# Gates in one go, 112 candidate sums, 896 dense columns: one change to the expert stage of a two-block transformer kernel

## The chip, the cores and the metric

The kernel runs on one core of a Trainium2 chip. A time is the device time of one execution in microseconds; a comparison uses the median of several executions on the same chip. The time before is 2967.11 us (median of 3 runs, 2965.75 to 2971.43). The profile comes from one more execution, of 2963.08 us, whose span from the first to the last instruction is 2961.3 us.

## The reference, cut to what matters

One sequence of 256 tokens, 2048 channels, goes through a mixer block, a gated feed-forward block, a second mixer, and then the part that is changed: a layer of 16384 experts, of which every token uses 8 heads x 16. Each expert is a row of `expert_u` and a row of `expert_v`.

```
s1, s2 = scores of 128 half keys each, per token and head
v1, i1 = top_k(s1, 16);  v2, i2 = top_k(s2, 16)
cand = v1[:, None] + v2[None, :]            # 256 sums
vs, ci = top_k(cand, 16)
eidx = i1[ci // 16] * 128 + i2[ci % 16];  gates = softmax(vs)
act  = gelu(expert_u[eidx] . x)             # 128 experts a token
h    = h + sum_k (act * gates)[k] * expert_v[eidx[k]]
h    = h + sigmoid(rms_norm(h) @ w_ple_gate) * (p @ w_ple_proj)
```

Both lists `v1` and `v2` are sorted, so a sum at place (i, j) has (i + 1)(j + 1) - 1 sums ahead of it that are no smaller, and only places with (i + 1)(j + 1) <= 16 can be among the 16 largest.

## The kernel before, in words

Everything is one program, written as generators ("lanes") that are stepped by the loops that issue the main products. The order in which a step issues its instructions is fixed when the program is built, and each engine runs its own instructions in that order. `lanes.step()` steps all five lanes; it is called once for each weight chunk (`next_chunk`) and in the waiting loops (`until`). `beside()` steps lanes 2 to 4 in the product that makes the queries. Weights come in chunks of 128 x 1024 through SP's queue into four buffers (`raw`); a chunk of the early and last products is split into a high and a low part by ACT (L349) and DVE (L350), a chunk marked `whole` is not.

The expert stage has four parts.

*Selection.* `topk` (L1586) runs twice, on lanes 2 and 3, one for the even and one for the odd heads. For a head, DVE finds the 16 best half keys of both kinds for both halves of the tokens (`top16`, L1569, on 128 scores), POOL forms the 16 x 16 sums of each token half (L1601), DVE finds the 16 best of 256 (`top16` again), POOL works out the two places from the index (L1606 to L1611), DVE compares them with a counting row (L1616), POOL multiplies by the indices (L1618), DVE sums (L1624), and POOL makes the row index (L1626 to L1628). ACT makes the exponentials of the gates of that head (L1620) and POOL scales them (L1633). `slots_` (L1636) copies the gates when all heads are done.

*The u rows.* `u_rows` (L1675) has POOL issue indirect loads (`gather`, L1661, issued at L1663) of 128 rows of `expert_u`, one row of 8 KB for each of 128 tokens, into 10 seats (4 in the second half of the tokens). DVE multiplies each with the normed token and sums (L1703). The first of these sums is issued when four heads are selected. There are 256 such loads.

*The spread of the weights.* `spots` (L1716) turns the 128 weights of a token and their indices into a dense 128 x 128 map with matmuls (L1762, L1794) and puts it into G (`put`, L1742, copies by ACT). For the second half of the tokens this is done in two halves of the map, 16 groups of 8 tokens each: the first before the dense product, the second beside it, with an accumulator pair shared by two groups.

*The v rows.* The columns of `expert_v` are cut in two. The first 1024 (`w_vd`) are done densely: 128 chunks of 128 rows, each with 8 matmuls against G (L1900). The other 1024 (`w_vs`) are gathered, 256 loads of 128 rows of 4 KB into 8 seats, and DVE adds each one, times its weight, to an accumulator `sacc` (L1840). `v_rows` (L1820) is on lane 4; in the dense loop it gets two steps a chunk, and a step issues up to two loads and one sum. Ahead of one of the steps POOL copies a column of the newest chunk (L1897), so POOL's loads wait there until that chunk has landed; a chunk's buffer is free only after this copy. At the end of each token half `turned` (L1809) transposes the sum (L1815) and DVE adds it to x (L1817): for the first half 8 steps later on lane 0, for the second half at once, within the step.

*The end.* After the dense loop DVE adds the dense sums to x (L1904); `x_block` (calling `part` and `x_square`) makes the high and low parts of the 8 dense column blocks (ACT L545, DVE L546, the squares ACT L563 and POOL L564); the product of `p` and `w_ple_proj` follows (`pp_done`, L1911); then the 8 gathered blocks are treated alike; then the last gate's product runs over the blocks 0 to 15 in that order, three matmuls for each block and output, and `g_done` (L1928) finishes and stores.

Of the kernel before, what the change touches and what calls it, by code (L numbers as in the profile page):

```python
# [6 lines left out]
F32 = mybir.dt.float32  # L7
# [5 lines left out]
OP = mybir.AluOpType  # L13
# [6 lines left out]
CH = 1024  # L20
GORD = [3, 2, 1, 0]
# [42 lines left out]
def layout(i):  # L64
# [161 lines left out]
def program(tc, A, out, stage=99, dbg=None):  # L226
# [90 lines left out]
    if stage > 3:  # L317
        add("w_pq", split=False)
        whole.update(range(len(order), len(order) + 128))
        add_kout("w_vd", 128, 0)  # L320
# [1210 lines left out]
    subk, qring, eg, ek, kk = cK(8, 2, 128), cK(4, T), cK(2, 128), cK(8, 2, 2, 16), cK(2, 128)  # L1531
    G.dma_start(subk.rearrange("p h s n -> p (h s n)"), A["subk"])
    sc = slab("sc").rearrange("p (t h s n) -> p t h s n", t=2, h=8, s=2)
    cT = Carve("cT")
    e1T, e2T, wT = sq[:, 0], sq[:, 1], acc_sq
# [50 lines left out]
    def topk(first):  # L1586

        cand, oh = cT(2, 16, 16), cT(2, 2, 16, 16)
        vv, ii, iif = cT(2, 2, 16), cT(2, 2, 16).bitcast(U32), cT(2, 2, 16)
        vs, ci, cf, c1, gs = cT(2, 16), cT(2, 16).bitcast(U32), cT(2, 16), cT(2, 2, 16), cT(2, 4)  # L1590
        xf = cT(2, 16)
        flat = lambda v: v.rearrange("p t s n -> p (t s n)")
        for h in range(first, 8, 2):
# [17 lines left out]
            G.tensor_add(c1[:, :, 1], c1[:, :, 1], cf)  # L1611
            G.tensor_scalar(gs[:, :, 0], vs[:, :, 0], -1.0, None, op0=OP.mult)
# [6 lines left out]
            for tt in range(2):  # L1619
                S.activation(eg[:, tt, hs], vs[:, tt], AF.Exp, bias=gs[:, tt, 0:1], accum_out=gs[:, tt, 1:2])  # L1620
# [4 lines left out]
            V.reciprocal(gs[:, :, 2], gs[:, :, 1])  # L1625
# [5 lines left out]
            for tt in range(2):  # L1631
                g = eg[:, tt, hs]
                G.tensor_scalar(g, g, gs[:, tt, 2:3], None, op0=OP.mult)  # L1633
            flags["heads"] = flags.get("heads", 0) + 1

    def slots_():  # L1636
# [3 lines left out]
        G.tensor_copy(gate_, eg)  # L1640
# [75 lines left out]
    def spots(tt):  # L1716
# [50 lines left out]
        else:  # L1767

            for half in range(2):
                lo, p = half * 64, None  # L1770
                for n in range(16):
# [18 lines left out]
                    if half == 0 or n % 2 == 0:  # L1790
                        p = pair("tok" if half else "sp")
                    at = 0 if half == 0 else n % 2 * 512
                    for k in range(8):
                        PE.matmul(p[:, at + k * 64:at + k * 64 + 64], Q[:, k], P[:, k, 0:64], start=True, stop=True)  # L1794
# [11 lines left out]
    vrow = [t.rearrange("p n d -> p (n d)").rearrange("p (n d) -> p n d", n=4)[:, j] for t in rows_[:2] for j in range(4)]  # L1806
    xb = {}

    def turned(t, tt, delay):  # L1809
# [3 lines left out]
        p = pair("tok")  # L1813
        for j in range(8):
            PE.transpose(p[:, j * 128:j * 128 + 128], t[:, j * 128:j * 128 + 128], ident)  # L1815
# [4 lines left out]
    def v_rows():  # L1820
# [4 lines left out]
        for n in range(256):  # L1825
# [16 lines left out]
            if s == 127:  # L1842
# [5 lines left out]
                if tt:  # L1848
                    for _ in turned(t, 1, 0):
                        pass  # L1850
# [104 lines left out]
```

## Time and profile before

| what | value |
|---|---|
| median of 3 runs | 2967.11 us |
| profiled execution, its span | 2963.08 us, 2961.3 us |
| PE busy | 2311.8 us, 78% |
| DVE busy | 1999.7 us, 68% |
| ACT busy | 1191.2 us, 40% |
| POOL busy | 900.9 us, 30% |
| moved from HBM | 757.77 MB |
| queue of SP's loads, of POOL's loads | 353.83 MB, 408.75 MB |

The expert stage takes the second half of the span, from about 1490 us on. Times in the rows are us from the span's start. A share of busy time is an average over stages with different limits; what bounds a stage is read from the windows of that stage (busy time of each engine, the granted TensorE clock, the DMA engines' share and rate) and from what ended the idle time before an instruction, which stands in brackets behind it. DMA share is the mean busy share of the 16 DMA engines. A fp32 matmul of 256 columns is recorded as two instructions.

### The profile page before, as it was taken

The page shows a single profiled execution, that of the slowest core. Times are in us where ns is not written, and L with a number is a line of the kernel's source. Part 1 is how long each engine was busy: PE and PEld are TensorE (multiplying, and loading weights), DVE is VectorE, ACT ScalarE, POOL GpSimd, SP SyncE. Part 2 cuts the span into 40 slices and gives each one's busy share as a digit, 9 for nine tenths or more (in the row PEclk, how much of TensorE's full clock was granted, in tenths as well). Part 3 has the DMA queues.
Part 4 walks back from the last instruction along what each step waited for, and adds up shares of the span by engine and source line. Part 5 has one row for each costly group of instructions (what it writes and reads, how often), then busy time and mean ns, then how long its engine had stood idle before and what let it go on. Part 6 is the DMA issues. An engine that isn't in the chain of part 4 may idle for free.

```text
span 2961.3 us, 39499 instructions
## 1 busy us (share of the span) xinstructions
PE 2311.8 (78%) x14635; PEld 2106.1 (71%) x14635; DVE 1999.7 (68%) x2615; ACT 1191.2 (40%) x2560; POOL 900.9 (30%) x1262
## 2 busy tenths in 40 slices
PE   8999999999999999999997200022222999999799
PEld 8887898888889999998986200011122988888689
DVE  5455666555556565656537999988998866666655
ACT  4355555444444454445411000058880444400043
POOL 3202215111111000331135543333334555555420
PEclk9999999999999999999998655555555799999999
DMA  6444455655655555543557799999997799999945
GB/s 221 153 128 122 134 158 180 196 188 187 197 187 190 185 180 184 172 151 109 182 201 279 291 407 422 422 397 408 415 415 317 265 403 404 395 401 409 366 148 166
DMA packets 174675, 765.11 MB, mean 258 GB/s; under 512 B 19585, under 2 KB 22049, under 8 KB 141201
## 3 DMA queue, kind: packets, MB, share of 16 engines
q1 hardware_dynamic: 99216, 353.83, 36.0%
q0 software_dynamic: 75264, 408.75, 34.5%
q8 instruction: 115, 1.88, 0.3%
q14 instruction: 80, 0.65, 0.1%
HBM read 757.77 MB, written 4.21 MB: 257 GB/s over the span
## 4 chain that ended last, share of the span: by engine, by line
PE 59%; DMA 12%; DVE 10%; issue 9%; POOL 8%; ACT 1%; another core or an unknown queue 0%; SPq 0%; POOLq 0%; DVEq 0%; ACTq 0%
PE acc L411 11%; PE acc L1900 7%; PE acc L386 6%; PE acc L388 6%; PE acc L387 6%; DMA rows<-w_vs,idx 6%; PE acc L412 6%; POOL rows L1663 5%; DMA rows<-w_u,idx 5%; DVE rows L1703 5%; PE acc L485 3%; PE acc L483 3%; PE acc L484 3%; PE sp L1794 1%; DMA raw<-w_vd 1%
## 5 line engine op out<-in xcount | busy, mean ns | idle before, releaser
L350 DVE TENSOR_TENSOR wlo<-raw,whi 128x1024 fp32r<-128x1024 f32 (+1 forms) x501 | 613.5, 1233 | 415.1 <-ACT whi L349 408.3
L349 ACT CAST whi<-raw 128x1024 fp32r<-128x1024 f32 (+1 forms) x501 | 519.7, 1042 | 380.2 <-PE acc L387 130.9
L1703 DVE SCALAR_TENSOR_TENSOR rows<-rows,yt 128x2048 f32<-128x2048 f32 x256 | 580.3, 2285 | 42.9 <-DMA rows<-w_u,idx 38.6
L1900 PE MATMUL acc<-G,raw 128*128 128x256 f32 x2048 | 457.3, 385 | 12.4 <-DMA raw<-w_vd 11.1
L1900 PEld LDWEIGHTS acc<-G,raw 128*128 128x128 f32 x2048 | 391.8, 193 | 71.7 <-DMA raw<-w_vd 17.0
L1840 DVE SCALAR_TENSOR_TENSOR sacc<-rows,sm,sacc 128x1024 f32<-128x1024 f32 x254 | 327.3, 1289 | 143.8 <-DMA rows<-w_vs,idx 127.4
L1663 POOL DMA_INDIRECT rows<-w_u,idx x256 | 244.2, 954 | 380.0 <-DVE rows L1703 274.8
L1663 POOL DMA_INDIRECT rows<-w_vs,idx x256 | 248.8, 972 | 149.6 <-DVE sacc L1840 81.7
L411 PE MATMUL acc<-xl,whi 128*128 128x512 f32 x704 | 248.2, 391 | 0.0
L411 PE MATMUL acc<-xh,whi 128*128 128x512 f32 x704 | 248.1, 391 | 0.0
L1762 PE MATMUL sp<-P,Q 128*128 128x128 f32 x256 | 60.2, 430 | 213.9 <-ACT P L1758 213.9
L1762 PEld LDWEIGHTS sp<-P,Q 128*128 128x128 f32 x256 | 55.8, 330 | 218.6 <-ACT P L1758 218.6
L564 POOL TENSOR_TENSOR acc_sq<-acc_sq,sq 128x256 f32<-128x256 f32 x63 | 57.0, 904 | 504.6 <-ACT sq L563 502.7
L485 PE MATMUL acc<-ring,wlo 128*128 128x256 f32 x704 | 199.3, 283 | 0.1
L483 PE MATMUL acc<-ring,whi 128*128 128x256 f32 x704 | 199.3, 283 | 0.1
L484 PE MATMUL acc<-ring,whi 128*128 128x256 f32 x704 | 199.2, 283 | 0.0
L412 PE MATMUL acc<-xh,wlo 128*128 128x256 f32 x704 | 197.2, 280 | 0.0
L412 PE MATMUL acc<-xl,wlo 128*128 128x256 f32 x704 | 197.1, 280 | 0.0
L1659 PE MATMUL yt<-keep,xg 128*128 128x128 f32 x32 | 5.6, 350 | 237.6 <-DVE rows L1703 237.1
L1191 POOL TENSOR_TENSOR hT<-cF 128x256 f32<-128x256 f32 x44 | 70.8, 1609 | 372.7 <-ACT whi L349 342.8
L1659 PEld LDWEIGHTS yt<-keep,xg 128*128 128x128 f32 x32 | 5.0, 184 | 238.1 <-DVE rows L1703 237.3
L386 PE MATMUL acc<-xh,whi 128*128 128x256 f32 x520 | 150.6, 290 | 3.2 <-ACT whi L349 1.8
(486 smaller groups left out, 5692.7 us busy)
## 6 DMA issues: line engine op xcount, KB each, us to landing
raw<-w_gu SPq DMA_DIRECT2D x176, 512.0 KB
raw<-w_vd SPq DMA_DIRECT2D x128, 512.0 KB
raw<-w_down SPq DMA_DIRECT2D x88, 512.0 KB
raw<-w_out SPq DMA_DIRECT2D x32, 512.0 KB
raw<-w_pq SPq DMA_DIRECT2D x32, 512.0 KB
raw<-w_pg SPq DMA_DIRECT2D x32, 512.0 KB
raw<-w_b SPq DMA_DIRECT2D x24, 512.0 KB
raw<-w_lat SPq DMA_DIRECT2D x18, 512.0 KB
```

The lines of the kernel that those rows point to most:

```text
L349: S.copy(hi[j][:, a:b], raw[j][:, a:b])
L350: V.tensor_sub(lo[j][:, a:b], raw[j][:, a:b], hi[j][:, a:b].bitcast(F32))
L386: PE.matmul(ps, wh, xh, start=start, stop=False, **k)
L411: PE.matmul(ps, wh, xh.both(k), start=k == 0, stop=False, skip_group_check=True)
L412: PE.matmul(ps[:, :T], wl, xh[:, k], start=False, stop=k == kb - 1, skip_group_check=True)
L483: PE.matmul(o, wh, ah, start=(k == 0 and j % 2 == 0), stop=False, skip_group_check=True)
L484: PE.matmul(o, wh, al, start=False, stop=False, skip_group_check=True)
L485: PE.matmul(o, wl, ah, start=False, stop=(k == nk - 1), skip_group_check=True)
L1663: G.indirect_dma_start(dst, None, src, bass.IndirectOffsetOnAxis(ap=idx[:, tt, s:s + 1], axis=0))
L1703: V.scalar_tensor_tensor(r, r, 1.0, accT, op0=OP.mult, op1=OP.mult, accum_out=wv[:, tt, s:s + 1])
L1840: V.scalar_tensor_tensor(sacc, r, w, sacc, op0=OP.mult, op1=OP.add)
L1900: PE.matmul(o, w, gs_[k // 16][:, k % 16], start=(k == 0 and j % 2 == 0), stop=k == 127, skip_group_check=True)
```

## The change

Three edits, with what they need around them.

- In `topk` the candidates are 112 sums instead of 256: the first 4 places of list 1 with all 16 of list 2, and places 4 to 15 of list 1 with the first 4 of list 2. They lie one behind the other, so POOL works out the two places from the index with more instructions. The exponentials leave `topk`: each head's 16 best sums stay in `vsa`, and `slots_` makes all gates at once.
- The dense part of `expert_v` has 896 columns (7 matmuls a chunk, chunks of 128 x 896), the gathered part 1152 (rows of 4608 bytes, 6 seats, an accumulator of three banks). The accumulator takes a bank from the pair that `spots` used in its second half, so there each group of 8 tokens has a bank and a `put` of its own.
- At the end of the second token half `turned` goes to lane 0 with a delay of 5 steps and then makes the parts of the gathered blocks (`finished`). After the dense loop, lanes 4 and 0 are finished first; the parts of the 7 dense blocks are made between the outputs of the `p` product; and the last gate's product runs over the blocks from 7 to 15 and then 0 to 6 (`Rolled`, with the rows of `w_ple_gate` rolled alike).

```diff
+KV = 7
+DV = KV * 128
+SV = 2048 - DV
-    a["w_vd"] = np.ascontiguousarray(i["expert_v_2"][0][:, :CH])
-    a["w_vs"] = np.ascontiguousarray(i["expert_v_2"][0][:, CH:])
-    a["w_pg"] = blocks(i["w_ple_gate_2"][0])
+    a["w_vd"] = np.ascontiguousarray(i["expert_v_2"][0][:, :DV])
+    a["w_vs"] = np.ascontiguousarray(i["expert_v_2"][0][:, DV:])
+    a["w_pg"] = blocks(np.roll(i["w_ple_gate_2"][0], -DV, axis=0))
...
             G.tensor_copy(iif, ii)
             for tt in range(2):
-                G.tensor_add(cand[:, tt], vv[:, tt, 0][:, :, None].to_broadcast([128, 16, 16]),
-                             vv[:, tt, 1][:, None, :].to_broadcast([128, 16, 16]))
+                for a, na, nb, at in ((0, 4, 16, 0), (4, 12, 4, 64)):
+                    G.tensor_add(cand[:, tt, at:at + na * nb].rearrange("p (a b) -> p a b", a=na), ...)
             yield
-            yield from top16([(cand[:, tt].rearrange("p a b -> p (a b)"), vs[:, tt], ci[:, tt]) for tt in range(2)])
+            vs = vsa[:, h]
+            yield from top16([(cand[:, tt], vs[:, tt], ci[:, tt]) for tt in range(2)])
             G.tensor_copy(cf, ci)
-            G.tensor_scalar(c1[:, :, 0], cf, 1.0 / 16, -7.5 / 16, op0=OP.mult, op1=OP.add)
-            G.tensor_scalar(c1[:, :, 0], c1[:, :, 0], 1.5 * 2.0 ** 23, None, op0=OP.add)
-            G.tensor_scalar(c1[:, :, 0], c1[:, :, 0], 1.5 * 2.0 ** 23, None, op0=OP.subtract)
-            G.tensor_scalar(c1[:, :, 1], c1[:, :, 0], -16.0, None, op0=OP.mult)
-            G.tensor_add(c1[:, :, 1], c1[:, :, 1], cf)
-            G.tensor_scalar(gs[:, :, 0], vs[:, :, 0], -1.0, None, op0=OP.mult)
+            i_, j_, r_ = c1[:, :, 0], c1[:, :, 1], 1.5 * 2.0 ** 23
+            G.tensor_scalar(i_, cf, 1.0 / 16, -7.5 / 16, op0=OP.mult, op1=OP.add)
+            G.tensor_scalar(i_, i_, r_, None, op0=OP.add)
+            G.tensor_scalar(i_, i_, r_, None, op0=OP.subtract)
+            G.tensor_scalar(j_, cf, 0.25, -12.375, op0=OP.mult, op1=OP.add)
+            G.tensor_scalar(j_, j_, r_, None, op0=OP.add)
+            G.tensor_scalar(j_, j_, r_, None, op0=OP.subtract)
+            G.tensor_scalar(far, cf, 1.0 / 112, -7.5 / 112, op0=OP.mult, op1=OP.add)
+            G.tensor_scalar(far, far, r_, None, op0=OP.add)
+            G.tensor_scalar(far, far, r_, None, op0=OP.subtract)
+            G.tensor_sub(j_, j_, i_)
+            G.tensor_mul(j_, j_, far)
+            G.tensor_add(i_, i_, j_)
+            G.tensor_scalar(xf, i_, 12.0, -48.0, op0=OP.mult, op1=OP.add)
+            G.tensor_mul(xf, xf, far)
+            G.tensor_scalar(j_, i_, -16.0, None, op0=OP.mult)
+            G.tensor_add(j_, j_, cf)
+            G.tensor_add(j_, j_, xf)
...
-            for tt in range(2):
-                S.activation(eg[:, tt, hs], vs[:, tt], AF.Exp, bias=gs[:, tt, 0:1], accum_out=gs[:, tt, 1:2])
...
-            V.reciprocal(gs[:, :, 2], gs[:, :, 1])
...
-            for tt in range(2):
-                g = eg[:, tt, hs]
-                G.tensor_scalar(g, g, gs[:, tt, 2:3], None, op0=OP.mult)
...
-        G.tensor_copy(gate_, eg)
+        G.tensor_copy(gs, ga[:, :, 0])
+        G.tensor_tensor(ga, ga, gs[:, :, None].to_broadcast(wide), op=OP.subtract)
+        yield
+        S.activation(ga, ga, AF.Exp)
+        for _ in range(2):
+            yield
+        V.tensor_reduce(gs, ga, axis=AX.X, op=OP.add)
+        V.reciprocal(gs, gs)
+        G.tensor_mul(gate_..., vsa, gs...)
...
-                    if half == 0 or n % 2 == 0:
-                        p = pair("tok" if half else "sp")
+                    p = bank(pairs_["tok"], "tok") if half else pair("sp")
...
-                    if half and n % 2:
-                        put(range(4, 8), t0 - 8, p, 16)
-                    elif not half:
-                        put(range(4), t0, p[:, 0:512], 8)
+                    put(range(4 * half, 4 * half + 4), t0, p[:, 0:512], 8)
...
+    def finished(which):
+        for j in which:
+            part(xb["h"][:, j], xb["l"][:, j], xb["x"][:, j], C("ple", j))
+            x_square(0 if j == KV else 1 + j % 2, xb["x"][:, j])
     def turned(t, tt, delay):
         for _ in range(delay):
             yield
-        p = pair("tok")
-        for j in range(8):
-            PE.transpose(...)
-        V.tensor_add(o, o, p.rearrange("p (k t) -> p k t", k=8))
+        for j0 in range(0, 16 - KV, 4):        # 4, 4 and 1 blocks, one bank
+            p = bank(pairs_["tok"], "tok")
+            for j in range(n):
+                PE.transpose(...)
+            V.tensor_add(o, o, p[:, :n * 128].rearrange("p (k t) -> p k t", k=n))
         yield
+        if tt:
+            finished(range(KV, 16))
...
-                    if m < 256 and m % 8 not in busy:
+                    if m < 256 and m % 6 not in busy:
...
-                if tt:
-                    for _ in turned(t, 1, 0):
-                        pass
-                else:
-                    lanes.add(0, turned(t, 0, 8))
+                lanes.add(0, turned(t, tt, 5 if tt else 8))
...
+    lanes.finish([4, 0])
...
+        if j % 2 and j // 2 < KV:              # in pp_done
+            finished([j // 2])
...
-    until("v")
-    for j in range(8, 16):
-        x_block(j, x, C("ple"), xh, xl)
...
-    project(16, 16, (xh, xl), g_done, ready=lambda: flags.get("n5"))
+    project(16, 16, (Rolled(xh), Rolled(xl)), g_done, ready=lambda: flags.get("n5"))
```

## Rows read from the trace of the kernel before

**Rows 1.** Windows: us, busy of PE, PEld, DVE, ACT, POOL, clock, DMA, GB/s

```profile
1594.00:1707.00 113.00, 44.90 (x189) 37.58 (x187) 103.76 (x261) 8.95 (x37) 59.18 (x113) 0.69 0.77 285
1707.00:2270.00 563.00, 64.11 (x273) 59.26 (x273) 520.05 (x457) 240.42 (x773) 208.61 (x223) 0.53 1.00 412
2270.00:2333.00 63.00, 56.41 (x257) 55.17 (x257) 50.03 (x50) 13.04 (x67) 42.38 (x40) 0.50 0.51 162
2333.00:2570.00 237.00, 233.77 (x1177) 207.62 (x1178) 163.40 (x136) 128.68 (x413) 126.19 (x179) 0.98 1.01 396
2570.00:2809.00 239.00, 220.09 (x1009) 189.28 (x1007) 157.75 (x124) 2.13 (x7) 123.03 (x180) 0.98 1.01 401
2841.00:2864.00 23.00, 18.67 (x136) 18.02 (x134) 20.06 (x30) 17.25 (x40) 9.09 (x12) 0.85 0.45 147
2864.00:2961.30 97.30, 90.08 (x737) 88.67 (x737) 59.37 (x82) 39.68 (x53) 7.54 (x19) 0.99 0.53 163
```

**Rows 2.** Costliest groups of the page: busy, mean ns | idle before, releaser

```profile
L1703 DVE SCALAR_TENSOR_TENSOR rows<-rows,yt 128x2048 f32<-128x2048 f32 x256 | 580.3, 2285 | 42.9 <-DMA rows<-w_u,idx 38.6
...
L1840 DVE SCALAR_TENSOR_TENSOR sacc<-rows,sm,sacc 128x1024 f32<-128x1024 f32 x254 | 327.3, 1289 | 143.8 <-DMA rows<-w_vs,idx 127.4
```

**Rows 3.** Chain of waits, four pieces: start, us, what

```profile
1702.11 88.33 DVE rows L1703 x80
...
1809.57 19.12 DMA rows<-w_u,idx
...
2341.21 13.87 PE acc L1900 x64
...
2678.57 13.68 DMA rows<-w_vs,idx
```

**Rows 4.** DVE in order of time, one head and the first row's sum

```profile
1559.83 0.85 DVE L1572 MAX8 cT<-sc 128x8 f32<-128x128 f32 x4
...
1567.99 0.74 DVE L1580 MAX8 cT<-cT 128x8 f32<-128x256 f32 x2
...
1571.62 1.22 DVE L1616 TENSOR_TENSOR cT<-cT,keep 128x1024 f32<-128x1024 f32 x1 [2.10 <-POOL cT L1611]
...
1594.08 2.27 DVE L1703 SCALAR_TENSOR_TENSOR rows<-rows,yt 128x2048 f32<-128x2048 f32 x1
```

**Rows 5.** POOL in order of time, the places of the same head

```profile
1569.59 0.21 POOL L1606 CAST cT<-cT 128x32 f32<-128x32 uint32 x1 [3.54 <-DVE cT L1583]
1569.89 0.22 POOL L1607 TENSOR_SCALAR cT<-cT 128x32 f32<-128x32 f32 x1
1570.20 0.30 POOL L1608 TENSOR_SCALAR cT<-cT 128x32 f32<-128x32 f32 x1
1570.59 0.29 POOL L1609 TENSOR_SCALAR cT<-cT 128x32 f32<-128x32 f32 x1
...
1571.34 0.25 POOL L1611 TENSOR_TENSOR cT<-cT 128x32 f32<-128x32 f32 x1
```

**Rows 6.** DVE in order of time, a later head, between two rows' sums

```profile
1642.08 2.27 DVE L1703 SCALAR_TENSOR_TENSOR rows<-rows,yt 128x2048 f32<-128x2048 f32 x1
...
1644.27 1.22 DVE L1616 TENSOR_TENSOR cT<-cT,keep 128x1024 f32<-128x1024 f32 x1
```

**Rows 7.** DVE and PE in order of time, from the last v row on

```profile
2806.12 2.62 DVE L1840 SCALAR_TENSOR_TENSOR sacc<-rows,sm,sacc 128x1024 f32<-128x1024 f32 x2 [1.10 <-DMA rows<-w_vs,idx]
...
2809.84 1.97 PE L1815 MATMUL tok<-keep,rows 128*128 128x128 f32 x8 [11.38 <-ACT rows L1847]
...
2811.60 29.77 PE L1900 MATMUL acc<-G,raw 128*128 128x256 f32 x128
...
2840.45 2.47 DVE L1904 TENSOR_TENSOR x<-x,acc 128x512 f32<-128x512 f32 x4
...
2842.84 6.56 DVE L546 SCALAR_TENSOR_TENSOR xh<-x,colt,xh 128x256 fp32r<-128x256 f32 x8
...
2848.70 0.58 PE L386 MATMUL acc<-pl,whi 128*128 128x256 f32 x1 [4.32 <-ACT pp L1912]
```

More of the change, by code (lines that the diff above doesn't have):

```diff
@@ L319, in program @@
         whole.update(range(len(order), len(order) + 128))
-        add_kout("w_vd", 128, 0)
+        for j in range(128):
+            order.append((A["w_vd"][j * 128:(j + 1) * 128], DV))
     if stage > 4:
@@ L1639, in slots_ @@
             yield
-        G.tensor_copy(gate_, eg)
+        for _ in range(2):
+            yield
+        wide = [128, 16, 16]
+        gs = kk.rearrange("p k n -> p (k n)")[:, 0:16]
+        G.tensor_copy(gs, ga[:, :, 0])
+        G.tensor_tensor(ga, ga, gs[:, :, None].to_broadcast(wide), op=OP.subtract)
+        yield
+        S.activation(ga, ga, AF.Exp)
+        for _ in range(2):
+            yield
+        V.tensor_reduce(gs, ga, axis=AX.X, op=OP.add)
+        V.reciprocal(gs, gs)
+        G.tensor_mul(gate_.rearrange("p t (h n) -> p h t n", h=8), vsa, gs.rearrange("p (h t) -> p h t", t=2)[:, :, :, None]
+                     .to_broadcast([128, 8, 2, 16]))
         for tt in range(2):
@@ L1803, in spots @@
         flags[("g", tt)] = True
-    vrow = [t.rearrange("p n d -> p (n d)").rearrange("p (n d) -> p n d", n=4)[:, j] for t in rows_[:2] for j in range(4)]
+    vflat = [t.rearrange("p n d -> p (n d)") for t in rows_[:2]]
+    vrow = [t[:, j * SV:j * SV + SV] for t in vflat for j in range(3)]
     xb = {}
+    def finished(which):
+        for j in which:
+            part(xb["h"][:, j], xb["l"][:, j], xb["x"][:, j], C("ple", j))
+            x_square(0 if j == KV else 1 + j % 2, xb["x"][:, j])
     def turned(t, tt, delay):
@@ L1828, in v_rows @@
                 for _ in range(2):
[L1829 to L1831 removed]
+                    if m < 256 and m % 6 not in busy:
+                        gather(vrow[m % 6], A["w_vs"], m)
+                        busy[m % 6] = m
                         m += 1
@@ L1834, in v_rows @@
                     yield
-            r, w = vrow[n % 8], wv[:, tt, s:s + 1]
+            r, w = vrow[n % 6], wv[:, tt, s:s + 1]
             if s == 0:
-                sacc = pair("sacc")
+                sacc = pairs_["sacc"].tile([128, 1536], F32, name="sacc", tag="sacc")[:, :SV]
                 V.tensor_scalar(sacc, r, w, None, op0=OP.mult)
@@ L1840, in v_rows @@
                 V.scalar_tensor_tensor(sacc, r, w, sacc, op0=OP.mult, op1=OP.add)
-            del busy[n % 8]
+            del busy[n % 6]
             if s == 127:
-                if tt:
-                    t = vrow[1]
-                else:
-                    t = gs_["t"] = hip.tile([128, CH], F32, name="tok", tag="whi")
-                S.copy(t, sacc)
-                if tt:
-                    for _ in turned(t, 1, 0):
-                        pass
-                else:
-                    lanes.add(0, turned(t, 0, 8))
+                t = vrow[1][:, :CH] if tt else hip.tile([128, CH], F32, name="tok", tag="whi")
+                t2 = vflat[tt][:, 3 * SV:3 * SV + SV - CH]
+                S.copy(t, sacc[:, :CH])
+                S.copy(t2, sacc[:, CH:])
+                t = [t[:, j * 128:j * 128 + 128] for j in range(8)] + [t2[:, j * 128:j * 128 + 128] for j in range(8 - KV)]
+                lanes.add(0, turned(t, tt, 5 if tt else 8))
             yield
@@ L1892, in program @@
                 part(pl[:, 0, j], pl[:, 1, j], pf[:, j], None)
-        for j in range(8):
-            w, _ = next_block()
-            if j == 0:
-                G.tensor_copy(xb["beat"], w[:, 0:1])
-                lanes.step_one(4)
+        w, _ = next_chunk()
+        G.tensor_copy(xb["beat"], w[:, 0:1])
+        lanes.step_one(4)
+        for j in range(KV):
             o = ps[j // 2][:, (j % 2) * T:(j % 2) * T + T]
-            PE.matmul(o, w, gs_[k // 16][:, k % 16], start=(k == 0 and j % 2 == 0), stop=k == 127, skip_group_check=True)
+            PE.matmul(o, w[:, j * 128:j * 128 + 128], gs_[k // 16][:, k % 16], start=(k == 0 and j % 2 == 0), stop=k == 127, skip_group_check=True)
     x, xh, xl = xb["x"], xb["h"], xb["l"]
+    st["blk"] = 8
     for i, q_ in enumerate(ps):
-        V.tensor_add(x[:, 2 * i:2 * i + 2], x[:, 2 * i:2 * i + 2], q_.rearrange("p (k t) -> p k t", t=T))
-    for j in range(8):
-        x_block(j, x, C("ple"), xh, xl)
+        o = x[:, 2 * i:min(2 * i + 2, KV)]
+        V.tensor_add(o, o, q_.rearrange("p (k t) -> p k t", t=T)[:, :min(2, KV - 2 * i)])
+    lanes.finish([4, 0])
     gt5 = xb["c"](4, T)
```

30 lines of the change are left out of this document (19 added, 11 removed).

## The prediction

> **What bounds the kernel now.** I read the windows by stage first, then the chain of waits, then the order of instructions on DVE and POOL where the change cuts in, and last the tail.
>
> The windows [rows 1] show three regimes. From 1594 to 1707 DVE is busy 103.76 of 113 us and the DMA engines only 0.77: selection and the u rows' sums share DVE. From 1707 to 2270 the DMA share is 1.00 at 412 GB/s while PE and POOL idle: the u rows are bound by bytes. DVE alone runs at first (88.33 us back to back in the chain), then the chain changes to DMA pieces [rows 3], because a row takes DVE 2.29 us [rows 2] and the DMA 128 x 8192 B / 0.42 = 2.5 us. The reader is to see that the bound of this stage starts only when selection lets DVE go: before 1707 no DMA backlog exists (0.77), so whatever delays or speeds the last head moves the whole rest of the u stage. From 2333 to 2809 DMA share is 1.01 at 396 and 401 GB/s, and PE is busy 233.77 of 237 and 220.09 of 239 us [rows 1]. The chain has PE pieces early and DMA pieces late [rows 3]: two limits almost level, and a cut of one of them alone gains only down to the other.
>
> **Part 1, selection.** Of its DVE work, ten instructions a head (max, find, replace, max and find, for each of two token halves) go from 256 to 112 elements. A MAX8 costs 0.85 / 4 = 0.21 us at 128 and 0.74 / 2 = 0.37 at 256 [rows 4], so 1.23 ns an element; 144 elements fewer is 0.177, ten of them 1.8 us a head. POOL's sums for the first comparison: two adds of 256 become four of 64 or 48. The nearest row for small operands is the 128 x 32 add of 0.25 us [rows 5]; four of about 0.3 replace two of 0.6, nothing.
>
> The places cost more. Before, from the cast to the end of the last needed instruction: 1569.59 to 1571.59, 2.0 us for six instructions [rows 5]. After there are 18: the cast (pitch 0.30), four two-operation scalars (0.31 each), seven one-operation scalars (0.38, the step from L1608 to L1609 with rounding) and six adds or multiplies (0.25 plus a gap of 0.07). That is 0.30 + 1.24 + 2.66 + 1.92, less the last gap, 6.05 us, so 4.05 more.
>
> Is it on the path? In an early head DVE has nothing else: it stands 2.10 us before L1616, released by POOL's L1611 [rows 4], which is the whole of POOL's 2.0. From the fifth head on a row's sum lies in front of L1616 and hides the 2.0 (it is 2.2 us long, and L1616 follows with no idle time) [rows 6], but it can't hide 6.05: 3.85 stay. So each head gains 1.8 on DVE and loses about 4.05 on POOL in the same serial chain, net +2.28; eight heads, +18.2 us. The row sums begin after the fourth head (1594.08 [rows 4]), 9 us later, and the last head ends 18 us later. Behind L1616 in DVE's order stand the next row's sum and, through its seat, POOL's next load, so the loads wait as well. What is late next is the byte-bound stage itself: with no backlog ahead of 1707, its end moves from 2270 by the same 18 us. Bounds: if the 4.05 were hidden by rows' sums and DVE's 1.8 all counted, 8 x -1.8 = -14; if each of the 12 new instructions took 0.38 and the wait of both came in full, +4.56 - 1.0 for a MAX8 gain half as large, +28. I take +18, nearest to the row that shows the wait whole.
>
> The gates: ACT's 16 exponentials, POOL's 16 scalings and eight reciprocals leave, one of each over 256 elements comes with a subtraction and a reduction. ACT is busy 8.95 of 113 us there and POOL 59.18 [rows 1]; behind the moved instructions stand only loads with full seats. ACT no longer stands before its exponentials, so queries and scores come sooner, but DVE's order of heads is fixed and doesn't wait for them. 0, and +2 if the reduction makes DVE wait once.
>
> **Part 2, the cut of the columns.** From 2270 to 2333 nothing but the length of a sum changes (0.125 us for 128 columns: 2285 less 1289 ns over 1024 [rows 2]) while PE is busy 56.41 of 63 at clock 0.50 [rows 1]: 0, at most +2.
>
> In the dense loop PE loses 128 of 1024 matmuls. Four chunks are a 13.87 us piece [rows 3], so a chunk goes from 3.47 to 3.03 us, 56 us in all. DMA gets more: 256 x 128 rows x 512 B is +16.78 MB, 128 x 128 rows x 512 B is -8.39 MB, net +8.39 MB. At the stage's mean of 398.5 GB/s [rows 1] that is +21.0 us, since the DMA share is 1.01 already. Per chunk: 1.573 MB in 3.95 us before, 1.638 MB in 4.11 us after, against PE's 3.03. DVE's two sums a chunk are 2.83. So PE's 56 us fall off the path, and the bytes stay. Bounds: 0, if the DMA would run faster beside an emptier PE; and for six seats instead of eight (3.54 MB under way instead of 4.19, against a piece of 13.68 us [rows 3] that holds a full ring) another +8. The extra puts of `spots` and the short waits on its one bank lie beside ACT (128.68 of 237 us busy) and PE's new slack: 0, +3 without that.
>
> The Trainium skill (DMA: Bandwidth & Descriptors, section Bandwidth) has about 358 GB/s as the limit of a core's HBM side; the windows show 396 to 412 sustained [rows 1], so the measurement decides. By the page the 8.39 MB would be 23.4 us.
>
> **Part 3, the tail.** Before, the last v sum ends at 2808.74; the transposes of the second half are issued inside the dense loop, so PE stands 11.38 us until ACT has copied the sum, then does them in 1.97 and needs 29.77 for the last eight chunks [rows 7]: 32.6 us from the last sum to the end of the dense loop. After, five more chunks precede the transposes. PE had done the chunk before them 10.3 us ahead of the last sum; with the same lead, five chunks (15.2) end 4.9 after it, nine transposes with two waits for DVE's adds take some 4.2, three chunks 9.1: 18.2 us, -14.4. The nine gathered blocks' parts (0.82 a block [rows 7]) run beside these last chunks; without that cover they cost up to 7.4. The moved step issues no DMA; POOL's adds of the squares go with it, and POOL is busy 9.09 of 23 us there [rows 1].
>
> Then the `p` product: it fills 2841 to 2864, with PE busy 18.67 of 23 and DVE 20.06 [rows 1], and PE waits 4.32 for ACT at one point [rows 7] because eight blocks' parts precede a copy. After, DVE has the four adds (2.47 [rows 7]), seven parts and the same copies and low parts: the window's 20.06 less about six parts of 0.82, 15 us. With ACT behind the nine parts I take 17: -6. The last product itself (90.08 us in its window [rows 1]) keeps its length; taking the gathered blocks first only removes waits for the late ones, which are already few. Sum -20; bounds -26 (all waits gone) and -5 (parts or low halves late, uncovered).
>
> **The sum.** +18.2 + 21.0 - 20.4 = +18.8 us on the profiled execution of 2963.08, so 2982. The median shown lies 4.0 us above that execution, so the forecast for a median is **2986 us**, 0.6% slower.
>
> **The rivals.**
> (a) *The bytes of the cut are free.* PE is busy 233.77 of 237 us in the first half of the loop [rows 1], and the chain runs through PE there [rows 3]; if PE sets that pace, an emptier PE lets the DMA run at the u stage's rate, 412 GB/s, which is most of what the bytes ask for. Against it: a DMA share of 1.01 and DMA pieces in the chain's second half. Then +18.2 + 0 - 20.4 = -2: 2965, no change.
> (b) *The selection gets shorter.* Place: heads five to eight, where a row's sum stands in front of L1616. DVE is 92% busy there, and if rows' sums cover POOL's longer chain, 1.8 us a head counts instead. For it: no idle time before L1616 [rows 6]. Against: 2.2 us of cover for 6.05. It decides from a growth of POOL's chain below 1.8 us a head (new instructions under 0.15 us, half of any row). Then -14.2 + 21.0 - 20.4 = -13.6: 2953, faster.
> (c) *PE's clock falls in the dense loop.* PE would wait 1.1 us in each chunk. The row of 2270 to 2333 shows 0.50, the 1.2 GHz level, after a stage in which PE was busy 64 of 563 us [rows 1]; a chunk at that level takes 6.07 us, above the 4.11 of the bytes, 1.96 more. If a third of the 66 chunks after `spots` ran so: +43, 3029. Against: 0.98 with PE's waits of the second half [rows 1], and a PE that is late is busy and gains the clock back. The Trainium skill (TensorE: Matmul & The Clock Gate, section HAM oscillation) describes this for products that wait for DMA at every tile. [...]
> (d) *Six seats starve the ring*, +8 more and a late tail: 3000.
>
> **How the numbers follow.** Forecast (POOL's chain exposed, bytes bind) 0.60, its own range 2972 to 3000; (a) 0.15; (b) 0.16; (c) 0.05; (d) 0.04. About 0.2%, 6 us, is what a measurement of this kernel can tell from no change. Faster by more: (b), and part of (a), where the tail's bound is -26: 0.21. Within: most of (a) and a little of the forecast's low end, 0.14. Slower: the rest, 0.65. For 8 in 10 the range must take in (a) and (b) and the forecast's upper bounds, 2952 to 3009.
>
> **What would show it.** Right: DVE's wait before L1616's comparison near 6 us in early heads and 3 to 4 in late ones, the first row's sum near 1603, the u stage's end near 2288; DMA share 1.0 to the last v sum and a loop of v rows 20 us longer, with PE at 75 to 88%; no stand of PE before the transposes, and 130 us from the last v sum to the end instead of 152. Wrong: a u stage that ends by 2270 (then part 1 fails), a DMA rate above 410 GB/s in the dense loop (part 2), PE's clock below 0.9 there (c), or nine parts that PE waits for (part 3).

## The result, and the profile after

The changed kernel takes 2983.98 us (median of 6 runs, 2981.17 to 2993.11) against 2966.43 us (6 runs, 2959.45 to 2971.43): a ratio of 1.0062, 95% interval 1.0043 to 1.0082, 18 us slower. The forecast was 2986 us. The profiled execution is the longest of the six (2993.11 us, span 2991.3), and 15.8 us of it lie before the changed code: the first MAX8 of the selection starts at 1535.0, before at 1519.2. PE is busy 16 us longer up to there; its 512-column matmuls in the unchanged first part, at 399 ns each instead of 391, account for 10 of them. So stages are compared from the first MAX8 of their own run on.

The windows of the changed kernel, the first five cut at the same events as [rows 1] (us, busy of PE, PEld, DVE, ACT, POOL, granted TensorE clock with 1.00 for 2.4 GHz and 0.50 for 1.2 GHz, DMA share, GB/s); the last one starts at the end of the dense loop:

```profile
1619.70:1742.00 122.30, 8.13 (x41) 6.77 (x39) 97.35 (x256) 2.00 (x6) 64.89 (x149) 0.55 0.64 227
1742.00:2303.00 561.00, 64.79 (x277) 59.74 (x277) 520.68 (x459) 241.38 (x776) 212.00 (x230) 0.54 1.00 413
2303.00:2366.00 63.00, 56.55 (x258) 55.51 (x259) 52.17 (x50) 13.48 (x68) 39.84 (x38) 0.50 0.53 164
2366.00:2606.00 240.00, 224.60 (x1099) 194.95 (x1098) 175.16 (x133) 131.75 (x441) 126.10 (x178) 0.97 1.02 408
2606.00:2857.00 251.00, 208.29 (x900) 168.61 (x899) 178.42 (x129) 2.86 (x12) 126.72 (x186) 0.97 1.02 405
2873.40:2891.00 17.60, 13.00 (x86) 12.85 (x86) 15.07 (x25) 11.55 (x26) 6.60 (x10) 0.81 0.49 139
```

In the first row, from the first row sum to the end of the selection, DVE stands (waits idle) 25 of 122 us, before 9 of 113. The second and third rows are as before. In the dense loop the DMA share is still 1.02, at a higher rate (408 and 405 GB/s, before 396 and 401), and PE now has slack in the second half. The clock around the `p` product is 0.81 (last row), before 0.85. The first product of the last gate shows where the `p` product ends, before and after:

```profile
2859.38 0.28 PE L386 MATMUL acc<-xh,whi 128*128 128x256 f32 x1
...
2892.38 0.28 PE L390 MATMUL acc<-xh,whi 128*128 128x256 f32 x1
```

From the end of the dense loop (2841.36 and 2873.58) to there it is 18.0 us before and 18.8 after: the `p` product did not get shorter. The window of 23 us that [rows 1] give it reaches into the last gate's product.

DVE in order of time, one early head, the first row's sum, and two late heads:

```profile
1588.15 0.44 DVE L1586 MAX8 cT<-cT 128x8 f32<-128x112 f32 x2
...
1595.08 1.23 DVE L1638 TENSOR_TENSOR cT<-cT,keep 128x1024 f32<-128x1024 f32 x1 [5.99 <-POOL cT L1634]
1599.20 1.22 DVE L1644 TENSOR_REDUCE cK<-cT 128x64 f32<-128x1024 f32 x1 [2.90 <-POOL cT L1640]
...
1619.72 2.28 DVE L1732 SCALAR_TENSOR_TENSOR rows<-rows,yt 128x2048 f32<-128x2048 f32 x1
...
1644.34 1.23 DVE L1638 TENSOR_TENSOR cT<-cT,keep 128x1024 f32<-128x1024 f32 x1 [6.65 <-POOL cT L1634]
...
1668.79 2.27 DVE L1732 SCALAR_TENSOR_TENSOR rows<-rows,yt 128x2048 f32<-128x2048 f32 x1
...
1674.87 1.23 DVE L1638 TENSOR_TENSOR cT<-cT,keep 128x1024 f32<-128x1024 f32 x1 [3.81 <-POOL cT L1634]
```

The MAX8 got shorter as forecast (two in 0.44 us, before 0.74 [rows 4]). In this early head the wait before the comparison grew from 2.10 to 5.99 us. In a late head with a row's sum in front it is 3.81 us (4.12 in one of three), in the fifth head, with none in front, 6.65. The fifth head had none in front before the change either:

```profile
1616.00 1.23 DVE L1616 TENSOR_TENSOR cT<-cT,keep 128x1024 f32<-128x1024 f32 x1 [2.46 <-POOL cT L1611]
```

Over all eight heads DVE waits 46.3 us before the comparison, before the change 13.5, in five of them. What it waits for is this chain on POOL:

```profile
1589.14 0.21 POOL L1616 CAST cT<-cT 128x32 f32<-128x32 uint32 x1 [2.19 <-DVE cT L1589]
1589.44 0.22 POOL L1618 TENSOR_SCALAR cT<-cT 128x32 f32<-128x32 f32 x1
1589.74 0.30 POOL L1619 TENSOR_SCALAR cT<-cT 128x32 f32<-128x32 f32 x1
1590.13 0.30 POOL L1620 TENSOR_SCALAR cT<-cT 128x32 f32<-128x32 f32 x1
...
1594.79 0.25 POOL L1634 TENSOR_TENSOR cT<-cT 128x32 f32<-128x32 f32 x1
```

18 instructions from 1589.14 to 1595.04: 5.90 us, before 2.0 for six [rows 5].

The two groups of the page that answer to [rows 2]: the u sum is the same, the v sum costs 133 ns more, and its idle time is nearly all owed to DMA (131.8 of 134.1).

```profile
L1732 DVE SCALAR_TENSOR_TENSOR rows<-rows,yt 128x2048 f32<-128x2048 f32 x256 | 580.5, 2285 | 40.3 <-DMA rows<-w_u,idx 36.3
L1875 DVE SCALAR_TENSOR_TENSOR sacc<-rows,sm,sacc 128x1152 f32<-128x1152 f32 x254 | 361.2, 1422 | 134.1 <-DMA rows<-w_vs,idx 131.8
```

The tail, PE and DVE in order of time from the last v sum on, where [rows 7] had a stand of 11.38 us before the transposes:

```profile
2855.24 1.42 DVE L1875 SCALAR_TENSOR_TENSOR sacc<-rows,sm,sacc 128x1152 f32<-128x1152 f32 x1 [1.11 <-DMA rows<-w_vs,idx]
...
2864.33 0.60 PE L1848 MATMUL tok<-keep,rows 128*128 128x128 f32 x4
...
2867.37 6.21 PE L1931 MATMUL acc<-G,raw 128*128 128x256 f32 x28
...
2870.22 6.08 DVE L550 SCALAR_TENSOR_TENSOR xl<-x,colt,xl 128x256 fp32r<-128x256 f32 x8
2876.23 1.21 DVE L354 TENSOR_TENSOR wlo<-raw,whi 128x1024 fp32r<-128x1024 f32 x1
2877.36 2.20 DVE L1937 TENSOR_TENSOR x<-x,acc 128x512 f32<-128x512 f32 x4
...
2878.18 0.55 PE L390 MATMUL acc<-pl,whi 128*128 128x256 f32 x1 [4.60 <-DVE x L1937]
```

That stand is gone, but a smaller one came: the sums of the dense blocks (L1937) are queued on DVE behind the gathered blocks' parts (L550) and a low half (L354), and PE waits 4.60 us for them.

The stages of every run, from its trace, in us. Heads 1-4: first MAX8 to first row sum. u: from there to the start of the last row sum. v: from there to the start of the last v sum. Tail: from there to the end of the span. The last columns are the median of the runs and the ratio to the kernel before on the same chip; the experiments ran on three chips, so kernels are compared by their ratios. One of the six runs of e7 took 6191 us; it is left out of its median and its ratio.

| kernel | heads 1-4 | u | v | tail | median us | ratio, 95% |
|---|---|---|---|---|---|---|
| before | 74.9 | 673.8 | 539.5 | 153.9 | 2966.43 | |
| after | 84.7 | 681.6 | 553.9 | 136.1 | 2983.98 | 1.0062 [1.0043, 1.0082] |
| e1_old_selection | 74.8 | 673.3 | 554.0 | 135.8 | 2968.16 | 0.9992 [0.9974, 1.0010] |
| e2_new_selection | 84.6 | 684.0 | 540.0 | 152.6 | 2991.95 | 1.0060 [1.0035, 1.0084] |
| e3_new_tail | 74.8 | 674.8 | 537.2 | 135.6 | 2951.48 | 0.9937 [0.9915, 0.9959] |
| e4_places_on_dve | 70.8 | 679.4 | 553.7 | 135.3 | 2971.06 | 0.9995 [0.9976, 1.0015] |
| e5_split_places | 64.8 | 673.6 | 541.4 | 135.7 | 2943.79 | 0.9911 [0.9889, 0.9933] |
| e6_pe_cut | 74.8 | 675.3 | 534.6 | 131.7 | 2941.07 | 0.9903 [0.9882, 0.9924] |
| e7_six_seats | 75.0 | 672.5 | 538.6 | 135.5 | 2946.18 | 0.9928 [0.9905, 0.9952] |
| e8_early_turn | 74.9 | 674.4 | 536.9 | 130.4 | 2943.48 | 0.9915 [0.9894, 0.9937] |
| e9_best | 64.8 | 674.5 | 536.6 | 130.2 | 2933.93 | 0.9889 [0.9869, 0.9910] |
| e10_pe_full | 74.8 | 677.3 | 555.9 | 136.8 | 2972.94 | 1.0013 [0.9999, 1.0027] |

After against before by stage: +9.8, +7.8, +14.4, -17.8, together +14.2; with the 15.8 before the first MAX8 that is the 30.0 between the two spans. The slower start is more likely this execution's than the change's: the stages alone give 1.0048 for the changed kernel and 0.9990 for e4, whose trace also has matmuls of 399 ns, both inside the measured intervals; with their later first MAX8 (9.9 us in e4) it would be 1.010 and 1.0024, both outside. Kernels that share a stage show its spread: u 672.5 to 677.3 with the old selection, v 536.6 to 541.4 with 1024 columns, all products and the new tail.

### The profile page after: what moved, and what is told of

It reads as the page before. It is cut to its first block, busy times and chain, and to the rows that moved or that the text cites. A ratio compares the mean times of both kernels' runs of the same rounds, so it can differ in the third digit from the quotient of the medians.

```text
span 2991.3 us, 39084 instructions
## 1 busy us (share of the span) xinstructions
PE 2278.8 (76%) x14381; PEld 2059.2 (69%) x14381; DVE 2021.9 (68%) x2613; ACT 1191.8 (40%) x2563; POOL 922.5 (31%) x1352
## 4 chain that ended last, share of the span: by engine, by line
PE 52%; DMA 17%; DVE 10%; issue 10%; POOL 9%; ACT 1%; POOLq 0%; SPq 0%; DVEq 0%; ACTq 0%
DMA rows<-w_vs,idx 11%; PE acc L415 11%; PE acc L390 6%; PE acc L392 6%; PE acc L391 6%; PE acc L416 5%; POOL rows L1692 5%; DMA rows<-w_u,idx 5%; DVE rows L1732 5%; PE acc L489 3%; PE acc L487 3%; PE acc L488 3%; DVE sacc L1875 2%; PE sp L1821 1%; PE acc L460 1%
## 5 line engine op out<-in xcount | busy, mean ns | idle before, releaser
L354 DVE TENSOR_TENSOR wlo<-raw,whi 128x1024 fp32r<-128x1024 f32 (+1 forms) x501 | 614.4, 1234 | 399.5 <-ACT whi L353 392.9
L1875 DVE SCALAR_TENSOR_TENSOR sacc<-rows,sm,sacc 128x1152 f32<-128x1152 f32 x254 | 361.2, 1422 | 134.1 <-DMA rows<-w_vs,idx 131.8
L1931 PE MATMUL acc<-G,raw 128*128 128x256 f32 x1792 | 415.2, 390 | 39.6 <-DMA raw<-w_vd 38.6
L1931 PEld LDWEIGHTS acc<-G,raw 128*128 128x128 f32 x1792 | 343.1, 195 | 105.6 <-DMA raw<-w_vd 58.5
L415 PEld LDWEIGHTS acc<-xl,whi 128*128 128x128 f32 x704 | 132.3, 188 | 33.0
```

The lines of the kernel that those rows point to most:

```text
L354: V.tensor_sub(lo[j][:, a:b], raw[j][:, a:b], hi[j][:, a:b].bitcast(F32))
L415: PE.matmul(ps, wh, xh.both(k), start=k == 0, stop=False, skip_group_check=True)
L1875: V.scalar_tensor_tensor(sacc, r, w, sacc, op0=OP.mult, op1=OP.add)
L1931: PE.matmul(o, w[:, j * 128:j * 128 + 128], gs_[k // 16][:, k % 16], start=(k == 0 and j % 2 == 0), stop=k == 127, skip_group_check=True)
```

## The experiments

Theory: three effects in series that add up, POOL's longer place chain (+18), the gathered bytes (+21) and the tail (-20). The first three kernels take the change apart.

**e1_old_selection**: the changed kernel with `topk`, `slots_` and their tiles as before.

```
-        cand, oh = cT(2, 112), cT(2, 2, 16, 16)
+        cand, oh = cT(2, 16, 16), cT(2, 2, 16, 16)
...                                   # six place instructions, a softmax per head
```

> The changed kernel with the selection of the kernel before (256 sums, six place instructions on POOL, a softmax per head); 896 dense columns and the new tail stay. Theory (POOL's longer place chain stands in the serial path of every head, and everything behind it only shifts): the u stage ends 17 to 18 us earlier against the first MAX8, the rest is unchanged, 2984 - 17.6 = 2966 us, which is the kernel before within 0.2%. Rival (the selection is covered by the rows' sums, and the loss lies in the bytes and the tail): 2980 us or more. A smaller rival: the byte-bound u stage catches up half of the late start: 2975.

2968.16 us, ratio 0.9992. Heads and u stage are those of before, v and tail those of after: bytes and tail all but cancel, and the loss goes with the selection.

**e2_new_selection**: the kernel before with the new `topk` and `slots_` alone (the reverse of the edit above).

> The kernel before with the selection of the changed kernel alone (112 sums, 18 place instructions on POOL, gates in one go); 1024 dense columns, eight seats and the old tail. Theory: +17 to 18 us, 2984 us, DVE's wait before the comparison 6.0 us in the early heads. Rival (covered by rows' sums): 2966 us or, by DVE's 1.8 us a head, 2953 us.

Ratio 1.0060, which is 17.8 us; in the trace heads +9.7, u stage +10.2, v +0.5 and tail -1.3. The rival that rows' sums cover the chain falls: DVE waits 46.1 us before the eight comparisons, against 13.5 before. The shorter searches, the longer chain and the gates in one go came together here; only e4 moves the chain alone.

**e3_new_tail**: e1 with 1024 columns on both sides.

```
-KV = 7
+KV = 8
-    vrow = [t[:, j * SV:j * SV + SV] for t in vflat for j in range(3)]
+    vrow = [t[:, j * SV:j * SV + SV] for t in vflat for j in range(4)]
...                                   # m % 8 and n % 8 for the seats; no t2
```

> The changed kernel with the old selection and with 1024 dense and 1024 gathered columns and eight seats, so that of the change only the new tail is left (transposes in a lane five steps after the last v sum, two groups of four; the gathered blocks' parts early; last product begun with them). Theory: last v sum to the end of the dense loop 21 to 22 us (five chunks of 3.47 less a lead of 10.3, some 4 for the transposes, three chunks 10.4) instead of 32.6, the p product 6 us shorter: 17 us, 2949 us. Rival (the tail gains only because the chunks are one matmul in eight shorter, and PE's stand of 11.4 us comes back elsewhere): 2960 us or more.

Ratio 0.9937, 18.7 us less, nearly all of it (18.3) after the last v sum. The sum came as expected, its split not: the dense loop ends 17.8 us after the last v sum (21 to 22 expected), and from there to the last gate's first product it is 17.6 us, before 18.0 (6 less expected), 3.32 of them a stand of PE. The narrower chunk wasn't needed for the gain. So the cut of the columns itself is the difference of e1 and e3: 0.0055, 16 us lost, 16.8 in the v stage of the traces.

**e4_places_on_dve**: the changed kernel with the places on DVE.

```
-            G.tensor_copy(cf, ci)
+            V.tensor_copy(cf, ci)
...                                   # the 17 instructions after it alike
```

> The changed kernel with the 18 place instructions of a head on DVE instead of POOL, nothing else. Theory: the price of the selection is the length of a chain of small dependent instructions on POOL (about 0.33 us each) with DVE standing; on DVE each should take about 0.1 us (an estimate from the 0.22 us of a MAX8 over 112 elements less its elements), so the chain is 2 to 3 us instead of 6 and needs no crossing: 3 to 4 us a head, 24 to 32 us off the changed kernel's 2984, 2952 to 2960. Rival (DVE has a fixed pitch near POOL's for dependent instructions, 0.3 us): DVE's time grows by 5.4 us a head also where rows' sums could have covered it, 2984 or slower. Rival (the byte-bound stage sets its own end): 2980.

Ratio 0.9995, 20 us under the changed kernel: less than forecast. DVE of the fourth head:

```profile
1591.14 0.18 DVE L1616 CAST cT<-cT 128x32 f32<-128x32 uint32 x1
1591.36 0.18 DVE L1618 TENSOR_SCALAR cT<-cT 128x32 f32<-128x32 f32 x1
...
1594.35 0.19 DVE L1634 TENSOR_TENSOR cT<-cT 128x32 f32<-128x32 f32 x1
1594.57 1.23 DVE L1638 TENSOR_TENSOR cT<-cT,keep 128x1024 f32<-128x1024 f32 x1
```

18 instructions take 3.4 us, 0.2 each, not the 0.1 that I had estimated. Heads 1-4 still fall by 13.9 us (3.5 a head), below even the kernel before; there the chain's length is the price. In the late heads less comes back: from the fourth to the eighth comparison it is 107.1 us before, 116.9 in the changed kernel and 112.0 here, and the u stage as a whole is only 2.2 us shorter, which is within its spread. That DVE, with rows' sums to do, pays there for each instruction that it takes over fits this, but no run shows it alone.

**e5_split_places**: e3, early heads on DVE and late ones on POOL.

```
+            E_ = V if h < 4 else G
-            G.tensor_copy(cf, ci)
+            E_.tensor_copy(cf, ci)
...                                   # the other six alike; for h < 4 also:
+                V.tensor_mul(o4, o4, iif...)   # 1024 elements, instead of four on POOL
```

> e3_new_tail with one edit: in the first four heads (before any row's sum, where DVE stands for POOL) the six places and the product with the indices run on DVE, in the last four they stay on POOL. Theory (the price of a selection step is the time DVE stands in the serial heads): a small DVE instruction took 0.20 us in e4_places_on_dve, so seven are 1.4 instead of a wait of 2.1, and one product of 1024 elements about 1.2 instead of a wait of 2.9; 0.7 + 1.7 = 2.4 us a head, first row sum 9.6 us earlier against the first MAX8, 0.9937 of the kernel before less 9.6 us: 0.9905. Rival (the loads of u rows aren't there 9.6 us earlier, since the byte-bound stage takes over): the row sums start earlier but the u stage ends within 4 us of where it ended: 0.993.

Ratio 0.9911, 7.7 us under e3 by the ratios (9.6 expected). Heads 1-4 take 64.8 us, 10.0 less, and the u stage keeps its length: the row sums start 10.0 us earlier and end 11.2 earlier. The v stage of this trace is 4.2 us longer than e3's, which no edit here explains; e9, with the same edit, doesn't have it. DVE runs from the comparison to the row sum without a stand:

```profile
1582.56 1.22 DVE L1621 TENSOR_TENSOR cT<-cT,keep 128x1024 f32<-128x1024 f32 x1
1583.82 1.22 DVE L1624 TENSOR_TENSOR cT<-cT 128x1024 f32<-128x1024 f32 x1
1585.08 1.22 DVE L1633 TENSOR_REDUCE cK<-cT 128x64 f32<-128x1024 f32 x1
1586.21 0.16 DVE L1634 RECIPROCAL cT<-cT 128x2 f32<-128x2 f32 x1
1586.28 2.27 DVE L1712 SCALAR_TENSOR_TENSOR rows<-rows,yt 128x2048 f32<-128x2048 f32 x1
```

**e6_pe_cut** and **e10_pe_full** ask what PE has to do with the price of the bytes. In e6 (from e3) the eighth product of chunks 1 to 126 is left out; in e10 (from e1) an eighth is added, into an unused half bank.

```
         for j in range(KV):          # e6
+            if j == 7 and 0 < k < 127:
+                continue
...
-        for j in range(KV):          # e10
+        for j in range(8):
-            PE.matmul(o, w[:, j * 128:j * 128 + 128], ...)
+            PE.matmul(o, w[:, j % KV * 128:j % KV * 128 + 128], ...)
```

> e3_new_tail with the eighth of the eight dense products of a chunk left out for chunks 1 to 126 (its block of columns is then not summed in full); bytes, seats and sums as they are. It asks whether the bytes of the cut cost less than 21 us because PE, emptier by one product in eight, lets the transfers run faster. Theory that PE holds the loop a little: v stage (last u sum to last v sum) 5 to 7 us shorter than e3's 537.2, the transfer rate up from 403 to about 408. Rival (PE's 56 us are wholly off the path): v stage within 1.5 us. In both the end after the last v sum is 2 to 3 us shorter, since fewer products are left there.

> e1_old_selection (896 dense columns, new tail, six seats) with an eighth product in each chunk, whose result is written to an unused half bank; so PE has the load of the kernel before and the bytes are those of the cut. It asks what in the cut's 14.4 us (forecast 21.0) is owed to PE's shorter chunks. Theory (a part): v stage 3 to 7 us longer than e1's 554.0, transfer rate over the loop 402 to 405 instead of 407, and 0.9992 of the kernel before plus these and some 4 us in the tail: 1.001 to 1.003. Rival (PE's load plays no role, the rate comes from the shapes of the transfers): v stage within 1.5 us.

The v stage is 2.6 us shorter in e6 than in e3, within the spread of like kernels, and 1.9 longer in e10 than in e1, where three kernels with 896 columns lie between 553.7 and 554.0. The windows of the first 47 or 48 us of the loop and of the whole loop, for e3, e6, e1 and e10 in this order (columns as above).

```profile
2337.00:2384.00 47.00, 46.57 (x226) 41.17 (x227) 35.01 (x30) 31.11 (x106) 25.03 (x36) 0.93 0.99 375
2337.00:2809.00 472.00, 463.16 (x2231) 404.52 (x2232) 320.54 (x260) 133.80 (x454) 249.03 (x359) 0.99 1.02 404
```

```profile
2338.00:2385.00 47.00, 46.72 (x230) 41.12 (x230) 35.87 (x31) 31.81 (x107) 26.41 (x38) 0.96 1.01 393
2338.00:2807.00 469.00, 427.44 (x1995) 363.35 (x1995) 319.46 (x260) 133.86 (x450) 249.62 (x359) 0.97 1.02 406
```

```profile
2332.00:2380.00 48.00, 47.99 (x236) 42.16 (x236) 36.40 (x29) 31.68 (x107) 26.70 (x38) 0.95 1.02 400
2332.00:2821.00 489.00, 434.74 (x1984) 365.45 (x1984) 352.12 (x261) 134.21 (x451) 251.79 (x361) 0.96 1.02 407
```

```profile
2340.00:2388.00 48.00, 47.63 (x233) 41.96 (x234) 37.44 (x29) 32.16 (x108) 26.17 (x38) 0.96 1.01 392
2340.00:2829.00 489.00, 464.44 (x2216) 401.62 (x2217) 351.45 (x260) 134.00 (x452) 252.50 (x360) 0.99 1.02 406
```

PE is full at the start in all four. With eight products a chunk the rate is 375 and 392 GB/s there, with seven 393 and 400, whichever the columns; over the whole loop 404 and 406 against 406 and 407. The other traces bear this out: over the first 47 us from the first dense product on, the seven kernels with 1024 columns and all products run at 372 to 383 GB/s, e6 at 392; the changed kernel runs at 398, e10 at 391. So PE's load holds the transfers back a little, at the start: 4% of 47 us, some 2 us. The theories' 3 to 7 us were too large, and the rivals' 1.5, by one trace each, a little too small: PE's 56 us are worth about 2. With PE's load kept, the cut costs 18.7 us in the v stage (e10 less e3).

**e7_six_seats**: e3 with `range(3)`, `m % 6` and `n % 6` as in the changed kernel.

> e3_new_tail with six seats for gathered v rows instead of eight, columns as they are (1024). Theory (the bytes bind; 3.15 instead of 4.19 MB under way are enough): v stage within 2 us of e3's 537.2, time within 2 us of it. Rival (the ring starves, the bound that the prediction kept at +8): v stage 8 us longer.

Ratio 0.9928, v stage 538.6 against 537.2: no starving with 3.15 MB under way. The changed kernel has more under way, 3.54, so rival (d) falls.

**e8_early_turn**: e3 with the transposes earlier.

```
-                lanes.add(0, turned(t, tt, 5 if tt else 8))
+                lanes.add(0, turned(t, tt, 3 if tt else 8))
```

> e3_new_tail with the transposes of the second half three steps behind the last v sum instead of five. Theory (the sums of the dense blocks wait on DVE behind the gathered blocks' parts, 3.32 us in which PE stands, after which its clock is at the lower level for some 6 us): the parts end before the dense loop does, the stand goes to under 1 us and the clock stays, 4 to 6 us off e3. Rival (PE reaches the transposes before ACT's copy of the sum, or the low halves come late instead): no gain, or 2 us lost.

Ratio 0.9915; the tail is 5.2 us shorter than e3's. The first product after the loop and the stretch of the p product, in e3 and in e8:

```profile
2831.91 0.55 PE L390 MATMUL acc<-pl,whi 128*128 128x256 f32 x1 [3.32 <-DVE x L1910]
...
2828.00:2845.00 17.00, 13.68 (x89) 13.31 (x88) 14.72 (x23) 11.29 (x25) 6.19 (x9) 0.80 0.50 147
```

```profile
2827.11 0.35 PE L390 MATMUL acc<-pl,whi 128*128 128x256 f32 x1 [0.17 <-DVE x L1910]
...
2826.00:2843.00 17.00, 16.83 (x137) 16.41 (x136) 15.89 (x27) 13.89 (x30) 6.75 (x8) 1.00 0.67 217
```

137 products instead of 89 fit into the 17 us from about the end of the dense loop on: the 48 more would take 5.8 us at 0.12 each; 3.3 of these are the stand itself, and the other 2.5 the clock. After the stand e3's products follow each other every 0.21 us until 2838 and every 0.12 from then on, and the granted clock of the stretch is 0.80, between the levels of 1.2 and 2.4 GHz; without the stand it is 1.00. From the end of the loop to the last gate's first product it is 11.8 us in e8, in e3 17.6.

**e9_best**: e5 and e8 together.

> e5_split_places and e8_early_turn in one kernel: 1024 dense and 1024 gathered columns, 256 sums, early heads' places and product on DVE, new tail with the transposes three steps behind the last v sum. Theory (stages in series, each gain shifts all that follows): e5 is 0.9911 of the kernel before and e8 0.9915, e3 between them and it 0.9928 to 0.9937; the gains of 5 to 7 us over e3 add up: 0.988 to 0.990, some 32 us under the kernel before. Rival (the early turn's gain is PE's clock, which depends on when the v stage ends): 0.991, no better than each alone.

2933.93 us, ratio 0.9889 [0.9869, 0.9910]: by the ratios 33 us under the kernel before and 51 under the changed one. Its heads are e5's and its tail e8's: in series, the gains add. It keeps of the change only the tail and the one-bank accumulator of `spots`.

## Why the prediction was right

- **Selection, forecast +18.2**: measured +17.6 in the trace of after (heads and u stage), +17.8 by e2's ratio and +19.9 in its trace. The mechanism held, head by head: the chain was forecast at 6.05 us and is 5.90, and from the third to the fourth comparison it is 17.13 us before and 19.39 after, +2.26 against a forecast of 2.28. The first row sum was to come 9 us later and comes 9.8 later. For late heads 3.85 of wait was forecast: it is 3.81 and 4.12 with a row's sum in front. The reading that from the fifth head on a row's sum always lies in front was wrong already for the kernel before, where the fifth head waits 2.46 us; its wait grew by 4.19. With the forecast's own 3.85 for the late heads its sum would have been 17.4.
- **Bytes, forecast +21.0**: this is the term that was most mis-sized. The v stage grew by 14.4 us, or 16.8 by e1 against e3. 8.39 MB did not move at the old mean of 398.5 GB/s on top of everything else: the rate of the loop went from 399 to 407 GB/s. About 2 us of the difference are PE's (e6 and e10). Two more may be the accumulators of `spots`: with 1024 columns the loop ran at 404 GB/s in e3 and in e9 with the new ones and at 400 in e2 with the old, but at 400 in e5 too, so this stays open, as does the rest. Of rival (a), bytes for free beside an emptier PE, the runs show these 2 us and no more.
- **Tail, forecast -20.4**: measured -17.8, by another split than forecast. The last v sum to the end of the dense loop is 16.9 us (forecast 18.2, before 32.6). The `p` product was 18.0 us long before, not the 23 that the prediction read from its window; forecast 6 us shorter, it is 0.8 longer: the stand of 4.60 us before it and the lower clock after it took the gain. The prediction had this as a bound (parts late) and as a sign against part 3 (PE waits for nine parts), and e8 removes it: there the stretch is 6.3 us shorter than before. The last product and the end, forecast unchanged, gave 3.0, 1.7 of them short waits of PE for DVE. From the end of the last v sum to the end of the span it is 134.6 us, 130 forecast, 152.6 before.
- **Rival (b)**, a shorter selection, falls with e2. A shorter selection can be had all the same: with the chain on DVE (e4) heads 1-4 do get shorter than before, by 4.1 us, and the late heads take it back.
- **Rival (c)**, PE's clock in the loop: 0.97 in both windows of the changed kernel, before 0.98. PE does wait for its chunk in the changed kernel, at 92 of 128 chunks and 97.0 us in all, each time about the 1.1 us that the prediction gives. Two chunks of e1 show it late in the loop; e1's clock over the loop is 0.96:

```profile
2799.58 3.29 PE L1906 MATMUL acc<-G,raw 128*128 128x256 f32 x14 [0.97 <-DMA raw<-w_vd]
2803.32 3.29 PE L1906 MATMUL acc<-G,raw 128*128 128x256 f32 x14 [0.45 <-DMA raw<-w_vd]
```

  The Trainium skill (TensorE: Matmul & The Clock Gate, section HAM oscillation) describes a loss of the clock in a loop where each wait for DMA is longer than the products between two waits. That isn't this loop, with waits of 1.05 us on average beside 3.29 us of products, and the clock stayed; a lower clock followed the longer stands of the tail, 3.32 us in e3 and 4.60 in the changed kernel.
- **PE's slack** was overrated: 75 to 88% busy was forecast, and it is 94% in the first half of the loop, where `spots` still runs, and 83% in the second. POOL, idle in the u stage by the prediction's words, is busy 208.61 of 563 us there [rows 1]; no term hangs on it.
- **The sum**: the stages of the traces add up to +14.2 us against a forecast sum of +18.8, and the medians differ by 17.6, with an interval of some 13 to 24 us. That the median came within 2 us of 2986 is in part luck: the bytes were put 6.6 too high, the tail's gain 2.6 too large, and the rest is the spread of executions.

## What to carry to other kernels

Before an engine's big instructions are made smaller, look at what its neighbour must add in return: 1.6 us less on DVE in an early head (3.9 less the net 2.26) was bought with 3.9 us of small dependent instructions on POOL, and in a serial stage the sum of both is what counts. Moving that work to DVE paid where DVE stood idle (13.9 us in the first four heads) and little where it had rows to sum. In a stage bound by bytes, columns that moved from a dense to a gathered product were paid mostly in bytes: the emptied engine's 56 us gave back about 2. And a step that is moved earlier to clear a stand should be checked for what it now stands in front of: three steps instead of five gave 5.2 us more, beside 18.3 for the tail in e3.

## What the runs showed of the hardware

- The 18 instructions of 128 x 32 elements follow each other every 0.25 to 0.39 us on POOL (changed kernel). On DVE (e4) it is 0.21 to 0.23 us where an instruction needs the result of the one before, and 0.09 to 0.11 where it doesn't.
- The core's transfers ran at 399 to 407 GB/s over whole loops and at 412 in the u stage. The Trainium skill (DMA: Bandwidth & Descriptors, section Specifications) gives about 358 as the limit of a core's HBM side; these runs, with one core at work, were above it, and the measurement decides.
- The unchanged first part of the kernel differs between the traces: 512-column matmuls of 399 ns in two (the changed kernel and e4) and of 391 or 392 in the other ten, and up to 15.8 us at the first MAX8, nearly as much as the effect under study. Only ratios over several runs, or times counted from an event of the same run, tell it apart.
